# Summing the last expert group in PSUM and normalising the other rows while its experts run

## The chip, the cores and the metric

The kernel runs on one core of one Trainium2 chip. The metric is the device time of one execution in microseconds (us): 941.54 us in the median of three runs of the kernel before (938.84 to 943.46).

The core has five engines with instruction streams of their own. TensorE (PE, with its weight loads as PEld) multiplies matrices into PSUM, VectorE (DVE) and ScalarE (ACT) work on tiles, GpSimd (POOL) issues the gathers, scatters and adding stores, and SyncE (SP) issues the plain loads and stores. Sixteen DMA engines move the data.

## The reference, cut to what matters

One decoder layer: a mixer sub-layer, which the change leaves alone, and then a mixture of experts. A router sends each of the 512 tokens to one of four groups and, inside it, to two of the group's four experts. The expert outputs are summed with their gates, added to the scaled input of the sub-layer, and normalised.

```python
for e in range(N_EXPERTS):                      # 16 experts, 4 in each group
    hid = jax.nn.silu(t @ w_gate[e]) * (t @ w_up[e])
    out = out + gates[:, e:e + 1] * (hid @ w_down[e])
...
y = hierarchical_moe(h, ...)
x = layer_norm(DEEPNORM_ALPHA * x + (1.0 + gt2) * y, ln2_g[l], ln2_b[l])
```

## The kernel before, in words

After the mixer and the router, `h2d` in HBM holds the experts' input by token, and `moed` holds the scaled residual, to which the expert results are added. `body(e, t)` runs tile `t` of up to 64 tokens (H) of expert `e`. Tile 0 is always run. Tiles 1 and 2 stand behind branches on the expert's token count, which each engine reads from SBUF into a register (`values_load`, a TENSOR_LOAD on every engine).

One body, in the order in which it stands on each engine: `up` (32 matmuls, L1281), `hidden` (Silu on ACT, L1285, and a product on DVE, L1286), then the `down` product of the tile before (16 matmuls, L1296), scaled by gate and modulation on DVE (L1300) and sent by `add` as an indirect DMA that adds to rows of `moed` (L1301, POOL). `x_columns` transposes the gathered tokens of the next expert (L1176, copied out by ACT, L1177), `hidden_columns` transposes the hidden tile (L1290, copied out by DVE), and `tile_tokens` turns one-hot rows (`onehots`, L1146, DVE) by small matmuls (L1151, L1153) into the token indices of expert `e + 2` and gathers their rows (L1156, POOL). `in_order` keeps PE, DVE and ACT in the order of the code inside one body: an instruction that waits holds up all that stand behind it on its engine.

Weights come over SP's queue (L358) into a ring of 1 MB buffers, some three experts ahead. A skipped branch that would have issued DMAs from POOL is made up for by an instruction on POOL that raises those DMAs' semaphores (INC_SWDGE_SEM).

At the end, the last `down` is added to `moed`. SP waits for that and loads all of `moed` back (L1420). For each of four tiles of 128 rows, DVE takes the statistics (L218, L219), ACT a square root (L220), DVE and ACT scale (L1424, L1425), and POOL stores to `out` with an adding DMA (L1426): `out` had been filled with the bias `ln2_b` in the middle of the mixer (L776).

Of the kernel before, what the change touches and what calls it, by code (L numbers as in the profile page):

```python
# [107 lines left out]
def hybrid_layer(ctx: ExitStack, tc: tile.TileContext, A, out):  # L108
# [663 lines left out]
    with tc.issue_after(ws.issued.ins):  # L772
# [3 lines left out]
        nc.sync.dma_start(out[0], bass.AP(tensor=A["ln2_b"].tensor, offset=A["ln2_b"].offset, ap=[[0, S], [1, D]]))  # L776
# [365 lines left out]
    rkx = rtile("rkx", [P, NT])  # L1142

# [68 lines left out]
    def over_counts():  # L1212
        nc.vector.tensor_copy(cnt, pc[:, 0:16])
        nc.vector.tensor_copy(cnti[:, 0:16], cnt)
        for b in range(NB):
            nc.vector.tensor_scalar(ext[:, b, :], cnt, float((b + INL) * H) + 0.5, None, op0=ALU.is_gt)
        nc.vector.tensor_reduce(nov, ext, axis=AX.XY, op=ALU.add)
        nc.vector.tensor_copy(cnti[:, 16:17], nov)

# [77 lines left out]

    def add(bank, yo, ix, gw):

        nc.vector.scalar_tensor_tensor(yo, bank, gw, gt2h, op0=ALU.mult, op1=ALU.mult)  # L1300
# [4 lines left out]
    def body(e, t):  # L1305

        bank, by, yo, sg = bgu[t], bys[t % 2], yos[t % 2], sgs[t % 2]
        with in_order((ET.PE, ET.DVE, ET.Activation)):
            if t == 0:
# [3 lines left out]
                tile_ranks(e, 2)  # L1313
            if t == 1:
                tile_tokens(e, 2)
# [7 lines left out]
            if t:  # L1323
                down(ew, e, by)
                add(by, yo, ixs[e % 3][t - 1], gws[e % 3][t - 1])
            elif e:
                down(ew, e - 1, by)
                add(by, yo, ixl[1 - e % 2], gwl[1 - e % 2])
                ew.drop(2)
# [3 lines left out]
            if t == 1:  # L1333
                x_columns(xgs[e % 2, 2], xTs[e % 2, 2])
            hidden_columns(sg)
            if t == 0 and e + 2 < NE:
                for u in range(2):
                    tile_tokens(e + 2, u)

    n_toks = [nc.values_load(cnti[0:1, e:e + 1], min_val=0, max_val=S) for e in range(NE)]  # L1340
    n_over = nc.values_load(cnti[0:1, 16:17], min_val=0, max_val=MAXO)
    n_raw = len(ew.raws)
    assert n_raw >= 18

    for e in range(NE):
        body(e, 0)
        with tc.If(n_toks[e] > H):  # L1347
            body(e, 1)
            with tc.If(n_toks[e] > 2 * H):
                body(e, 2)  # L1350
        if e + 1 < NE:
            ew.drop(4)
    down(ew, NE - 1, bys[0])
    add(bys[0], yos[0], ixl[(NE - 1) % 2], gwl[(NE - 1) % 2])


    spare = [ew.piece(6 * (NE - 3) + n) for n in range(18)]
    ms, gs = ([spare[6 + 2 * a + i // 2][:, i % 2 * D:(i % 2 + 1) * D] for i in range(NT)] for a in range(2))
    ln2g = spare[10][:, 0:D]
    nc.sync.dma_start(ln2g, row_bcast(A["ln2_g"], D))  # L1360
# [52 lines left out]
    with ExitStack() as nest:  # L1413
        for t in range(MAXO):
            nest.enter_context(tc.If(n_over > t))
            over(t)


    for i in range(NT):
        nc.sync.dma_start(ms[i], moed[i * P:(i + 1) * P, :])  # L1420
    for i in range(NT):
        mv = ln_stats(ms[i], f"y{i}")
        nc.vector.tensor_scalar(mv[:, 3:4], mv[:, 0:1], -1.0, None, op0=ALU.mult)
        nc.vector.scalar_tensor_tensor(gs[i], ms[i], mv[:, 3:4], ln2g, op0=ALU.add, op1=ALU.mult)  # L1424
        nc.scalar.mul(gs[i], gs[i], mv[:, 2:3])  # L1425
        nc.gpsimd.dma_start(out[0, i * P:(i + 1) * P, :], gs[i], accum_op=ALU.add)  # L1426
# [25 lines left out]
```

## Time and profile before

| | |
|---|---|
| median of three runs | 941.54 us |
| the profiled execution | 941.18 us |
| its span, first to last instruction | 939.3 us |
| PE busy | 845.4 us (90%) |
| DVE busy | 534.7 us (57%) |
| ACT busy | 313.6 us (33%) |
| POOL busy | 105.8 us (11%) |
| mean granted clock of TensorE | 0.958 |

The span runs from the first to the last instruction of the profiled execution, and the 1.9 us between it and the execution's own time lie around it. Busy shares are means over stages of different kinds: until 901 us PE works almost without a break, and in the last 38 us it does nothing. The granted clock is given as a share of TensorE's full clock: 1.00 is 2.4 GHz and 0.50 is 1.2 GHz.

### The profile page before, as it was taken

Reading aid. Unit: us, or ns where it says so; the run is one execution under the profiler, and the core shown is the slowest. Engines: PE = TensorE matmul, PEld = TensorE weight load, DVE = VectorE, ACT = ScalarE, POOL = GpSimd, SP = SyncE. Lnnn points to the kernel's source line nnn. Section 1 sums busy time; section 2 is a strip of 40 time slices with the busy share of each in tenths; the row PEclk is TensorE's granted clock in tenths of the full one; section 3 lists DMA queues with packets and bytes.
Section 4 is the critical chain, followed back from the end, with each engine's and each line's share of the span. In section 5 each row is a group of like instructions: output and inputs, shape, how many; then the busy total and the mean of one; then the engine's idle time right before and its main releaser. Section 6 shows DMA issues by size and latency. Waiting matters only on the chain. (4 is left out here: it accounts for less than half of the span.)

```text
span 939.3 us, 11850 instructions
## 1 busy us (share of the span) xinstructions
PE 845.4 (90%) x4216; PEld 544.4 (58%) x4216; DVE 534.7 (57%) x1310; ACT 313.6 (33%) x561; POOL 105.8 (11%) x118
## 2 busy tenths in 40 slices
PE   2899989999999999999999994999999999999830
PEld 1678768887666677878888882433344333334310
DVE  6849879858876678876845773422342223232123
ACT  5438787454644433423234351101111000011002
POOL 1001000000000000000000022222231222121111
PEclk9899999999999999999999975999999999999975
DMA  9951456313125258894424399598799997549445
GB/s 288 339 142 52 154 175 183 90 35 102 46 68 161 90 169 267 247 291 147 176 94 178 135 348 381 210 375 290 273 388 387 381 359 273 189 136 367 155 123 103
DMA packets 137409, 196.46 MB, mean 209 GB/s; under 512 B 11802, under 2 KB 85706, under 8 KB 137312
## 3 DMA queue, kind: packets, MB, share of 16 engines
q1 hardware_dynamic: 126848, 174.28, 54.5%
q0 software_dynamic: 10304, 21.08, 9.1%
q8 instruction: 46, 0.75, 0.3%
q14 instruction: 35, 0.29, 0.1%
q10 hardware_dynamic: 176, 0.06, 0.0%
HBM read 190.61 MB, written 15.25 MB: 219 GB/s over the span
## 5 line engine op out<-in xcount | busy, mean ns | idle before, releaser
L398 PE MATMUL bank<-rm,rm 128*128 128x512 f32 x512 | 206.1, 406 | 0.4 <-ACT rm L431 0.4
L400 PE MATMUL bank<-rm,rm 128*128 128x512 f32 x512 | 205.9, 402 | 0.0
L399 PE MATMUL bank<-rm,rm 128*128 128x512 f32 x512 | 205.1, 401 | 0.2 <-DVE rm L433 0.2
L1281 PE MATMUL bank<-bm,fm 128*64 128x512 f32 x472 | 124.2, 597 | 1.8 <-PEq L1347 0.8
L234 DVE TENSOR_TENSOR rm<-fm,rm 128x1024 fp32r<-128x1024 f32 (+1 forms) x76 | 87.5, 1162 | 43.2 <-ACT rm L233 27.6
L398 PEld LDWEIGHTS bank<-rm,rm 128*128 128x128 f32 x512 | 97.8, 191 | 22.1 <-issue 3.1
L399 PEld LDWEIGHTS bank<-rm,rm 128*128 128x128 f32 x512 | 97.3, 190 | 21.7 <-issue 2.1
L400 PEld LDWEIGHTS bank<-rm,rm 128*128 128x128 f32 x512 | 97.2, 190 | 20.7 <-issue 2.3
L1286 DVE TENSOR_TENSOR fm<-fm,bank 64x512 f32<-64x512 f32 x24 | 16.6, 692 | 152.2 <-ACT fm L1285 143.2
L233 ACT CAST rm<-fm 128x1024 fp32r<-128x1024 f32 (+1 forms) x76 | 75.1, 1008 | 78.4 <-PE bank L399 59.4
L1281 PE MATMUL bank<-fm,fm 128*64 128x512 f32 x296 | 81.4, 610 | 3.8 <-issue 1.9
L1285 ACT ACTIVATE fm<-bank 64x512 f32<-64x512 f32 x24 | 14.1, 589 | 198.6 <-PE bank L1281 198.6
L1281 PEld LDWEIGHTS bank<-bm,fm 128*64 128x64 f32 x472 | 38.1, 136 | 66.7 <-issue 65.4
L1296 PE MATMUL bank<-bm,fm 128*64 128x512 f32 x232 | 60.4, 592 | 0.0
L390 DVE SCALAR_TENSOR_TENSOR fm<-fm,cact,fm 128x256 f32<-128x256 f32 x112 | 51.2, 479 | 1.8
L1177 ACT COPY fm<-bank 128x512 f32<-128x512 f32 x38 | 20.9, 588 | 87.9 <-PE bank L1176 87.7
L1281 PEld LDWEIGHTS bank<-fm,fm 128*64 128x64 f32 x296 | 24.7, 140 | 40.7 <-issue 39.0
L1300 DVE SCALAR_TENSOR_TENSOR fm<-bank,fm,fm 128x512 f32<-128x512 f32 x24 | 18.0, 750 | 47.7 <-PE bank L1296 42.7
L1002 PE MATMUL bank<-rm,rm 128*128 128x512 f32 x192 | 44.2, 391 | 0.3 <-ACT fm L847 0.3
L1301 POOL DMA_INDIRECT moed<-fm,rt_ixl x16 | 25.6, 1603 | 152.5 <-DVE fm L1300 143.1
L1156 POOL DMA_INDIRECT fm<-h2d,rt_ix x38 | 39.1, 1029 | 28.7 <-DVE fm L1160 20.6
L1002 PEld LDWEIGHTS bank<-rm,rm 128*128 128x128 f32 x192 | 36.0, 188 | 8.1 <-ACT fm L847 0.7
(312 smaller groups left out, 1102.7 us busy)
## 6 DMA issues: line engine op xcount, KB each, us to landing
bm<-in_w_down SPq DMA_DIRECT2D x20, 1024.0 KB, 13.7
bm<-in_w_up SPq DMA_DIRECT2D x20, 1024.0 KB, 12.3
bm<-in_w_gate SPq DMA_DIRECT2D x20, 1024.0 KB
fm<-in_w_in SPq DMA_DIRECT2D x36, 512.0 KB, 4.9
fm<-in_w_mod SPq DMA_DIRECT2D x16, 1024.0 KB, 5.3
fm<-in_w_up SPq DMA_DIRECT2D x12, 1024.0 KB, 16.1
fm<-in_w_down SPq DMA_DIRECT2D x12, 1024.0 KB, 14.4
fm<-in_w_gate SPq DMA_DIRECT2D x12, 1024.0 KB
```

Of the source, the lines that this page charges most:

```text
L233: ins = nc.scalar.copy(hi, src)
L234: nc.vector.tensor_tensor(lo, src, hi.bitcast(F32), op=ALU.subtract)
L390: nc.vector.scalar_tensor_tensor(acc, r, cact[:, k:k + 1], acc, op0=ALU.mult, op1=ALU.add)
L398: nc.tensor.matmul(pt, whi[:, k, :], ah.ap, start=(k == 0), stop=False)
L399: nc.tensor.matmul(pt, whi[:, k, :], al.ap, start=False, stop=False)
L400: nc.tensor.matmul(pt, wlo[:, k, :], ah.ap, start=False, stop=(k == nk - 1))
L1002: nc.tensor.matmul(wps[i][hf], sta.ap[:, tsl], mov.ap[:, hf * 512:(hf + 1) * 512], start=(k == 0 and sta is mh and mov is wh), stop=(k == ...
L1156: nc.gpsimd.indirect_dma_start(out=xg, out_offset=None, in_=h2d2, in_offset=bass.IndirectOffsetOnAxis(ap=ix[:, 0:1], axis=0), bounds_check ...
L1177: nc.scalar.copy(xT, pt)
L1281: nc.tensor.matmul(bank[n * H:(n + 1) * H], xT[:, (2 * (k % 4) + k // 4) * H:(2 * (k % 4) + k // 4 + 1) * H], w, start=(k == 0), stop=(k = ...
L1296: nc.tensor.matmul(bank[n * H:(n + 1) * H], hidT[0][:, k, :], w, start=(k == 0), stop=(k == 3))
L1301: nc.gpsimd.indirect_dma_start(out=moed2, in_=yo, in_offset=None, compute_op=ALU.add, out_offset=bass.IndirectOffsetOnAxis(ap=ix[:, 0:1], ...
```

## The change: what it does

A flag `n_one` is counted beside the others: no expert needs more than three tiles, and the last group (experts 12 to 15) has at most 128 tokens. After expert 11 every engine branches on it (L1571). Where it is 0, `general()` runs what was there before, except that the bias is added by DVE and `out` is written by plain stores. Where it is 1, `Rows` runs experts 12 to 15 in another way:

- `begin` clears two PSUM banks (two matmuls with a zero matrix) and makes one-hot rows of the group's tokens. `slots` multiplies these with an expert's one-hot rows into a 0/1 matrix from expert slots to group slots. `sum` multiplies it with the scaled expert output, so that the four experts' results add up in the two banks. These experts send nothing to `moed`.
- Before expert 14, `load` puts the rows of `moed`, the gain, the bias, and a gather of the group's own rows on POOL's queue. `norm` normalises two tiles of 128 rows at the start of expert 14's body and two at the start of expert 15's, and SP stores them to `out` plainly. The group's rows among them are wrong at that point.
- After expert 13, `end` makes `ixg`, the token indices of the group's rows, by five small matmuls and two operations on DVE.
- `ends` adds the banks to the group's gathered rows in two halves of 512 columns (on DVE, with the row sums), squares them (ACT), takes the square root (ACT), applies gain and bias by halves (DVE), and stores them over the others with one indirect DMA.

The early store of the bias to `out` goes. `x_columns` uses one PSUM bank in these experts, where two alternated, and the tiles are at most two for an expert.

```diff
-        nc.sync.dma_start(out[0], bass.AP(tensor=A["ln2_b"].tensor, offset=A["ln2_b"].offset, ap=[[0, S], [1, D]]))
...
+        nc.vector.tensor_scalar(one[:, 0:1], nov, 0.5, None, op0=ALU.is_le)
+        nc.vector.tensor_scalar(one[:, 1:2], cnt[:, 19:20], P + 0.5, one[:, 0:1], op0=ALU.is_le, op1=ALU.mult)
+        nc.vector.tensor_copy(cnti[:, 17:18], one[:, 1:2])
...
-                tile_ranks(e, 2)
+                if not rows:
+                    tile_ranks(e, 2)
-            if t == 1:
+            if rows:
+                rows.start(e, t)
+            elif t == 1:
                 tile_tokens(e, 2)
...
+                if summed:
+                    weigh(by, yo, gw)
+                else:
+                    add(by, yo, ix, gw)
...
-                for u in range(2):
-                    x_columns(xgs[1 - e % 2, u], xTs[1 - e % 2, u])
+                x_columns(xgs[1 - e % 2, 0], xTs[1 - e % 2, 0])
+                if rows:
+                    hidden_columns(sg)
+                x_columns(xgs[1 - e % 2, 1], xTs[1 - e % 2, 1])
...
+            if rows:
+                if summed:
+                    rows.sum(yo)
+                rows.slots(t)
...
+        def begin(self):
+            for a in (zerob, *slot):
+                nc.vector.memset(a, 0.0)
+            nc.vector.tensor_scalar(itg, itf, 1.0, None, op0=ALU.add)
+            onehots(self.ohg, rk[:, :, 19], itg)
+            for bank in self.acc:
+                nc.tensor.matmul(bank, zerob, self.ohg.rearrange("p c s -> p (c s)"), start=True, stop=False)
+        def start(self, e, t):
+            if (e, t) == (self.first, 0):
+                self.begin()
+            onehots(ohs[3 + t], rk[:, :, e], itbs[t])
+            if t == 0 and e >= NE - 2:
+                for i in (2 * (e - NE + 2), 2 * (e - NE + 2) + 1):
+                    self.norm(i)
+        def slots(self, t):
+            pt = bix[:, 256:256 + P]
+            for c in range(NT):
+                nc.tensor.matmul(pt, ohs[3 + t][:, c, :], self.ohg[:, c, :], start=(c == 0), stop=(c == NT - 1))
+            for hf in range(2):
+                nc.scalar.copy(slot[hf][hf * H:(hf + 1) * H], pt[hf * H:(hf + 1) * H])
+        def sum(self, yo, last=False):
+            for hf in range(2):
+                nc.tensor.matmul(self.acc[hf], slot[hf], yo, start=False, stop=last)
+...
+        def load(self):
+            for i in range(NT):
+                nc.gpsimd.dma_start(self.zs[i], moed[i * P:(i + 1) * P, :])
+            nc.gpsimd.dma_start(self.lng, row_bcast(A["ln2_g"], D))
+            nc.gpsimd.dma_start(self.lnb, row_bcast(A["ln2_b"], D))
+            nc.gpsimd.indirect_dma_start(out=self.x1, out_offset=None, in_=moed[:, :],
...
+        def norm(self, i):
+            z, v = self.zs[i], mvr[:, i, :]
+            nc.scalar.activation(self.junk, z, AF.Identity, accum_out=v[:, 0:1])
+            nc.vector.tensor_scalar(v[:, 1:2], v[:, 0:1], -1.0 / D, None, op0=ALU.mult)
+            nc.scalar.activation(self.junk, z, AF.Square, bias=v[:, 1:2], accum_out=v[:, 2:3])
+            nc.scalar.activation(v[:, 3:4], v[:, 2:3], AF.Sqrt, bias=epsc, scale=1.0 / D)
+            nc.vector.scalar_tensor_tensor(z, z, v[:, 1:2], self.lng, op0=ALU.add, op1=ALU.mult)
+            nc.vector.reciprocal(v[:, 4:5], v[:, 3:4])
+            nc.vector.scalar_tensor_tensor(z, z, v[:, 4:5], self.lnb, op0=ALU.mult, op1=ALU.add)
+            nc.sync.dma_start(out[0, i * P:(i + 1) * P, :], z)
+        def ends(self):
+            nc.scalar.activation(mvr[:, 2, 3:4], epsc, AF.Sqrt)
+            down(ew, NE - 1, by)
+            weigh(by, yo, gwl[(NE - 1) % 2])
+            self.sum(yo, True)
...
+            nc.gpsimd.indirect_dma_start(out=out[0], out_offset=bass.IndirectOffsetOnAxis(ap=ixg[:, 0:1], axis=0),
+                                         in_=y, in_offset=None, bounds_check=S - 1, oob_is_err=False)
...
+    for e in range(NE - 4):
+        expert(e, INL)
+    with tc.If(n_one > 0) as last:
...
+            tr.tiles = banks[3:4]
+            for e in range(NE - 4, NE):
+                if e == NE - 2:
+                    rows.load()
+                expert(e, 2, rows)
...
+                rows.ends()
+    with last.Else():
+        general()
```

The order in which instructions stand changes at three places. A row below names the line, the operation, what it writes and what it reads; `fm_` and `bm_` are buffers, `bank_` PSUM banks.

On DVE, between the last instruction of expert 11 (the copy of its hidden columns) and the Silu product of expert 12, this stood before:

```order
L1291 COPY fm_70<-bank_66 128x256
L1349 UNCONDITIONAL_BRANCH x2
L1347 UNCONDITIONAL_BRANCH
L1146 TENSOR_SCALAR fm_70<-fm_80 128x128 x5
L1286 TENSOR_TENSOR fm_78<-fm_78,bank_61 64x512
```

and stands now (L1298 is the copy, L1149 the one-hot rows, L1293 the product):

```order
L1298 COPY fm_70<-bank_66 128x256
L1375 UNCONDITIONAL_BRANCH x3
L1367 TENSOR_LOAD rt_cnti x4
L1368 TENSOR_LOAD rt_cnti
L1369 TENSOR_LOAD rt_cnti
L1571 COMPARE_AND_BRANCH
L1149 TENSOR_SCALAR fm_70<-fm_80 128x128 x8
L1474 MEMSET fm_80 128x64
L1474 MEMSET fm_80 128x128 x2
L1475 TENSOR_SCALAR fm_80<-itf 128x128
L1149 TENSOR_SCALAR fm_70<-fm_80 128x128 x8
L1293 TENSOR_TENSOR fm_78<-fm_78,bank_61 64x512
```

The six register loads, four of which stood at the later branches, now precede the branch, and of the last eight one-hot rows the first four are the group's, for which PE's two clearing matmuls (L1478) wait ahead of `up` of expert 12.

On POOL, the gathers of expert 15's tokens, then the branch of expert 13, stood so before:

```order
L1301 DMA moed<-fm_78,rt_ixl_3500 1280x512
L1156 DMA fm_75<-h2d,rt_ix_3491 128x512
L1156 DMA fm_74<-h2d,rt_ix_3492 128x512
L1340 TENSOR_LOAD rt_cnti
L1347 COMPARE_AND_BRANCH
```

and stand so now (ISA is the raising of a semaphore, L1511 the loads of `moed`):

```order
L1604 ISA
L1159 DMA fm_75<-h2d,rt_ix_3490 128x512
L1604 ISA
L1159 DMA fm_74<-h2d,rt_ix_3491 128x512
L1375 COMPARE_AND_BRANCH
L1375 UNCONDITIONAL_BRANCH x2
L1604 ISA
L1511 DMA fm_77<-moed 128x1024
L1604 ISA
L1511 DMA fm_77<-moed 128x1024
L1604 ISA
L1511 DMA bm_3752<-moed 128x1024 x2
```

The loads of `moed` stand behind the second gather, and each of the first three behind one more raise; gain, bias and the gather of the group's rows follow them.

On ACT, expert 14 had its Silu and the two copies of the columns of expert 15, ahead of the next branch:

```order
L1285 ACTIVATE fm_78<-bank_61 64x512
L1177 COPY fm_75<-bank_65 128x512
L1177 COPY fm_74<-bank_64 128x512
L1340 TENSOR_LOAD rt_cnti
L1347 COMPARE_AND_BRANCH
```

and has now, from the end of expert 13's branch on (L1520 to L1523 are `norm`, L1292 the Silu, L1180 the copies, L1494 those of `slots`):

```order
L1520 ACTIVATE bm_3754,fm_80<-fm_77 128x1024
L1522 ACTIVATE bm_3754,fm_80<-fm_77,fm_80 128x1024
L1523 ACT_TABLE_LOAD
L1523 ACTIVATE fm_80<-fm_80,epsc 128x1
L1520 ACTIVATE bm_3754,fm_80<-fm_77 128x1024
L1522 ACTIVATE bm_3754,fm_80<-fm_77,fm_80 128x1024
L1523 ACTIVATE fm_80<-fm_80,epsc 128x1
L1292 ACT_TABLE_LOAD
L1292 ACTIVATE fm_78<-bank_61 64x512
L1180 COPY fm_75<-bank_64 128x512
L1520 ACTIVATE bm_3754,fm_80<-bm_3752 128x1024
L1180 COPY fm_74<-bank_64 128x512
```

The Silu of expert 14 now stands behind the statistics of two tiles of `moed` and two loads of ACT's function table.

## Rows read from the trace of the kernel before

**Rows 1.** Fifty us: length, busy us (x instructions), granted clock, DMA share, GB/s.
```profile
850.00:900.00 50.00, 45.64 (x230) 19.59 (x228) 12.96 (x48) 6.61 (x11) 10.59 (x8) 1.00 0.65 231
```
**Rows 2.** Timeline of the end: start, us, engine, line, what, idle time before.
```profile
897.76 3.65 PE L1296 MATMUL bank<-fm,fm 128*64 128x512 f32 x16 [0.71 <-DVEq L1347]
...
902.55 0.75 DVE L1300 SCALAR_TENSOR_TENSOR fm<-bank,fm,fm 128x512 f32<-128x512 f32 x1 [4.97 <-DMA moed<-fm,rt_ixl]
...
913.43 1.29 DVE L218 BATCH_NORM_STATS2 st_y<-bm 128x6 f32<-128x512 f32 x2 [10.13 <-DMA bm<-moed]
...
925.93 0.85 POOL L1426 DMA_DIRECT2D out<-bm  x1 [0.85 <-ACT bm L1425]
```
**Rows 3.** Line 1448, the program's end: ns min/median/max, first and last start.
```profile
L1448 SPq DRAIN  x3: 7/7/7, 934.7 to 938.7; - x3
```
**Rows 4.** Windows of ACT's line 1285, the Silu, from 842.4 us on.
```profile
842.40:939.30 96.90, 2.35 (x4) 0.83 0.63 186
```
**Rows 5.** PE's line 681: products with 128 x 128 weights, 512 columns.
```profile
L681 PE MATMUL bank<-fm,ones 128*128 128x512 f32 x2 | 1.0, 592 | 0.0
```
**Rows 6.** Groups of ACT, shapes apart: shape, count, busy us, mean ns, idle before.
```profile
L1177 ACT COPY fm<-bank 128x512 f32<-128x512 f32 x38 | 20.9, 588 | 87.9 <-PE bank L1176 87.7
...
L1018 ACT ACTIVATE fm<-fm,mv 128x1024 f32<-128x1024 f32 x6 | 6.9, 1154 | 24.5 <-DVE mv L1017 24.5
...
L1019 ACT ACTIVATE mv<-mv,epsc 128x1 f32<-128x1 f32 x6 | 1.8, 294 | 0.2
...
L1285 ACT ACT_TABLE_LOAD x1 | 1.3, 1283 | 6.7 <-issue 6.7
...
L1018 ACT ACTIVATION_READ_ACCUMULATOR fm<-fm,mv 128x1 f32 x6 | 1.1, 184 | 0.0
```
**Rows 7.** A group of DVE, columns as in rows 6.
```profile
L1424 DVE SCALAR_TENSOR_TENSOR bm<-bm,mv_y,bm 128x1024 f32<-128x1024 f32 x4 | 5.1, 1274 | 0.0
```
**Rows 8.** DMA issues of the whole span: count, KB each, median us to landing.
```profile
moed<-fm POOLq DMA_DIRECT2D x4, 512.0 KB, 4.9
...
moed<-fm,rt_ixl POOLq DMA_INDIRECT x16, 8.1
```
**Rows 9.** Timeline at the start of expert 12, columns as in rows 2.
```profile
842.16 0.42 DVE L1291 COPY fm<-bank 128x256 f32<-128x256 f32 x1 [0.26 <-PE bank L1290]
...
842.54 6.65 PE L1281 MATMUL bank<-fm,fm 128*64 128x512 f32 x29 [0.42 <-PEq L1349]
...
842.92 0.91 DVE L1146 TENSOR_SCALAR fm<-fm 128x128 bf16<-128x128 bf16 x5 [0.34 <-DVEq L1349]
```
**Rows 10.** Line 1340, the register loads: ns min/median/max, first and last start.
```profile
L1340 DVEq TENSOR_LOAD <-rt_cnti x16: 299/304/554, 594.8 to 897.1; - x16
```
**Rows 11.** DVE's timeline at a branch with one such load.
```profile
883.97 0.74 DVE L1146 TENSOR_SCALAR fm<-fm 128x128 bf16<-128x128 bf16 x4 [0.71 <-PEq L1347]
```
**Rows 12.** PE's timeline at an earlier stop, after the routing.
```profile
579.10 2.09 PE L1176 MATMUL bank<-ident,fm 128*128 128x128 f32 x8 [10.66 <-DMA fm<-h2d,rt_ix]
581.12 5.91 PE L1281 MATMUL bank<-fm,fm 128*64 128x512 f32 x17
```
**Rows 13.** Windows around changes of the granted clock, columns as in rows 1.
```profile
905.00:906.00 1.00, 0.00 (x0) 0.00 (x0) 0.00 (x0) 0.00 (x0) 0.14 (x1) 0.85 0.55 33
...
582.00:584.00 2.00, 2.00 (x8) 0.71 (x6) 0.48 (x3) 1.42 (x3) 0.00 (x0) 0.50 1.03 392
...
586.00:588.00 2.00, 2.00 (x12) 0.71 (x10) 1.42 (x7) 0.00 (x0) 0.00 (x0) 1.00 0.17 61
```
**Rows 14.** PE's timeline in expert 14: first matmuls, columns of expert 15.
```profile
869.63 1.07 PE L1281 MATMUL bank<-bm,fm 128*64 128x512 f32 x2
...
881.26 1.09 PE L1176 MATMUL bank<-ident,fm 128*128 128x128 f32 x8
```
**Rows 15.** POOL's timeline: the last gather of expert 15.
```profile
871.54 1.00 POOL L1156 DMA_INDIRECT fm<-h2d,rt_ix  x1 [0.31 <-DVE fm L1146]
```
**Rows 16.** Line 1347, the branches: POOL's raises of semaphores, ns min/median/max.
```profile
L1347 POOLq INC_SWDGE_SEM  x10: 1043/1298/2027, 595.0 to 897.9; - x10
```

More of the change, by code (lines that the diff above doesn't have):

```diff
@@ L1142, in hybrid_layer @@
     rkx = rtile("rkx", [P, NT])
+    zerob, itg = rtile("zerob", [P, P], BF16), rtile("itg", [P, P], BF16)
+    slot = [rtile(f"slot{hf}", [P, P]) for hf in range(2)]
+    ixg, mvr = rtile("ixg", [P, 1], I32), rtile("mvr", [P, NT, 5])
+    ixf = rtile("ixf", [P, 1])
     def onehots(oh, ranks, slots):
@@ L1338, in body, with expert @@
                     tile_tokens(e + 2, u)
+            if rows:
+                rows.end(e, t)
     n_toks = [nc.values_load(cnti[0:1, e:e + 1], min_val=0, max_val=S) for e in range(NE)]
     n_over = nc.values_load(cnti[0:1, 16:17], min_val=0, max_val=MAXO)
+    n_one = nc.values_load(cnti[0:1, 17:18], min_val=0, max_val=1)
     n_raw = len(ew.raws)
     assert n_raw >= 18
[L1345 to L1350, printed above, removed]
+    def expert(e, tiles, rows=None):
+        body(e, 0, rows)
+        with ExitStack() as nest:
+            for t in range(1, tiles):
+                nest.enter_context(tc.If(n_toks[e] > t * H))
+                body(e, t, rows)
         if e + 1 < NE:
             ew.drop(4)
[L1353 to L1357 removed]
+    assert rtc[1] <= 4 * UNIT
+    spare = [ew.piece(6 * NE - 18 + n) for n in range(18)]
     ms, gs = ([spare[6 + 2 * a + i // 2][:, i % 2 * D:(i % 2 + 1) * D] for i in range(NT)] for a in range(2))
[L1359 to L1360 removed]
+    ln2g, lnb = spare[10][:, 0:D], spare[11][:, 0:D]
     rtc[:] = spare[10][:, D:2 * D], 0
@@ L1411, in over, with general @@
         add(bys[1], yos[1], ixs[0][0], gws[0][0])
[L1413 to L1426, printed above, removed]
+    def general():
+        for e in range(NE - 4, NE):
+            expert(e, INL)
+        nc.sync.dma_start(ln2g, row_bcast(A["ln2_g"], D))
+        down(ew, NE - 1, bys[0])
+        add(bys[0], yos[0], ixl[(NE - 1) % 2], gwl[(NE - 1) % 2])
+        with ExitStack() as nest:
+            for t in range(MAXO):
+                nest.enter_context(tc.If(n_over > t))
+                over(t)
+        nc.sync.dma_start(lnb, row_bcast(A["ln2_b"], D))
+        for i in range(NT):
+            nc.sync.dma_start(ms[i], moed[i * P:(i + 1) * P, :])
+        for i in range(NT):
+            mv = ln_stats(ms[i], f"y{i}")
+            nc.vector.tensor_scalar(mv[:, 3:4], mv[:, 0:1], -1.0, None, op0=ALU.mult)
+            nc.vector.scalar_tensor_tensor(gs[i], ms[i], mv[:, 3:4], ln2g, op0=ALU.add, op1=ALU.mult)
+            nc.vector.scalar_tensor_tensor(gs[i], gs[i], mv[:, 2:3], lnb, op0=ALU.mult, op1=ALU.add)
+            nc.sync.dma_start(out[0, i * P:(i + 1) * P, :], gs[i])
@@ new lines, in arm @@
+    @contextmanager
+    def arm():
+        state = ew.nload, ew.ndrop, tr.tiles, tr.i
+        yield
+        ew.nload, ew.ndrop, tr.tiles, tr.i = state
+    for e in range(NE - 4):
+        expert(e, INL)
+    with tc.If(n_one > 0) as last:
+        with arm():
+            rows = Rows()
+            tr.tiles = banks[3:4]
+            for e in range(NE - 4, NE):
+                if e == NE - 2:
+                    rows.load()
+                expert(e, 2, rows)
+            with in_order((ET.PE, ET.DVE, ET.Activation)):
+                rows.ends()
```

77 lines of the change are left out of this document (61 added, 16 removed).

## The prediction, made before the changed kernel had run

> **What bounds the kernel now.** I read the stages first. In the window from 850 to 900 us PE is busy for 45.64 of 50 us, and the other engines for far less [rows 1]: as long as the experts run, the time is what PE does and each stop of PE. Then I read the timeline of the end. PE's last `down` begins at 897.76 and ends at 901.41; the product that weighs it waits until 902.55 for the adding store before it; the statistics start at 913.43, after an adding store and a load of all rows; the last store to `out` is issued at 925.93 [rows 2]. SP's drain, which waits for that store to land, comes at 934.7, and the span ends at 939.3 [rows 3]. So 37.9 us lie behind PE's last matmul: 24.5 to the issue of the last store, 8.8 to its landing, 4.6 for the program's end. Last I asked which side of the branch runs: from 842.4 us on there are four Silu [rows 4], so each of the experts 12 to 15 ran tile 0 alone, with at most 64 tokens. Each token has two experts in its group, so the group has at most 4 x 64 / 2 = 128 tokens, and the new path is taken.
>
> **The tail, the gain.** From PE's last matmul on, the new chain is: weigh 0.75, which no adding store holds up now, with 0.10 to start; two products of `sum`, 0.59 each [rows 5], to 1.95; bank plus residual by halves on DVE, each like the weighing, 0.75 [rows 2], to 3.4; the square of a half on ACT, half of 1.15 and 0.18 for its sum, to about 4.3; a load of ACT's function table, 1.28, since the Silu of expert 15 stands between the early Sqrt and this one, and the Sqrt itself, 0.29, to 5.9 [rows 6]; reciprocal and two halves of a product, 1.27 together [rows 7], to 7.5. Then POOL stores. So 24.5 becomes 7.5: -17.0. The store is 512 KB, not adding; the plain 512 KB write of POOL's queue landed in 4.9 us, the indirect adding one in 8.1 [rows 8]. I take 4.9, being plain, in place of 8.8: -3.9; with 8.1 it is -0.7. The 4.6 of the end stay. Together -20.9, bounds -17.7 and (the table load hidden, the chain 2 us shorter) -24.
>
> **The entry, a cost.** Expert 12's first matmul is at 842.54, just behind the last instruction of expert 11, and DVE's five one-hot rows (0.91 for five, 0.18 each) are beside it [rows 9]. Now PE's two clearing matmuls stand ahead of `up` and need the group's one-hot rows. On DVE come first six register loads, of 0.30 each by themselves [rows 10]; DVE's gap at a branch is 0.71 with one such load [rows 11] and 0.34 without [rows 9], so 0.37 each, 2.2. Then eight one-hot rows 1.5, three small clears and one operation about 0.6, four more one-hot rows 0.75, and the clearing, about 0.4: from 842.58, where the copy ends, to 848.0, and `up` at 848.5. +6.0; with overlapped register loads 3.5, with each step a little longer 7.
>
> A stop of PE costs a second time. At the end the granted clock was 0.85 in the microsecond from 905 on, four after the last matmul; after an earlier stop of 10.66 us [rows 12] it was 0.50 from 582 to 584 and 1.00 from 586 on [rows 13]. At the low level 17 matmuls took 5.91 us [rows 12], at the full one 29 took 6.65 [rows 9], 0.229 each: 17 would take 3.9, and the part of the low stretch ahead of them loses a little over 1. So +3.1 for a stop of 6 us, and nothing if the clock holds through it.
>
> **Experts 12 and 13, a cost.** Each has four matmuls for `slots` with their copies on ACT into the matrix, ahead of the matmuls of `tile_tokens`, which use the same bank (`bix`): about 0.45 on PE, and about 0.9 until both copies are done. The second `x_columns` waits for the copy of the first out of the one bank, 0.59 [rows 6], of which most but not all lies beside the hidden columns; 0.85 with the signals. That is +2.2 in expert 12. Expert 13 has the two products of `sum` too, 1.0, and five matmuls for `ixg`, 0.5: +3.7. Together +5.9; 3 if PE finds all copies done, 8 if each is waited for.
>
> **Expert 14, the largest cost.** Let S be PE's first matmul of expert 14, 869.63 before. The columns of expert 15 follow at 881.26, eight transposes in 1.09 [rows 14]; in the new order the hidden columns of expert 14 come after four of them, at S + 12.2. They need its Silu, and on ACT that stands behind the sums, squares and roots of two tiles of `moed`. When can these be done? POOL issued the last gather for expert 15 at 871.54, for 1.00 [rows 15], so it was free at S + 2.9. In the new listing one raise more stands between the two gathers and one behind them, of 1.30 each [rows 16]: 5.5, less 0.5, since PE's matmuls for `ixg` put S off against the gathers. So the first load of `moed` is issued at S + 5.0 and lands, by the 4.9 of rows 8, at 9.9. Four more issues of 0.9 and two raises of 1.3 later the gain is issued, at 11.2, and lands at 16.1, the bias at 17.0. ACT has summed (1.15 + 0.18) and squared (the same) the first tile by then [rows 6]. DVE waits for the gain: product 1.27 [rows 7], reciprocal, product with the bias, to 18.9. Only then comes its small product with the second tile's sum, which ACT's next square needs: 19.1, square to 20.4, root 20.7, table load for Silu 22.0, Silu 22.6, product 23.3. PE stops from 12.2 to 23.4, or 11.2; with raises at their least, 1.04 [rows 16], and issues that overlap, about 10. I take +10.0. Were gain and bias there as early as the tiles, 4; with loads that land in 8.1 and not in 4.9, 13. The clock then costs again, about 2.8. The two tiles of expert 15 (their data landed long before) need some 7 us, and its Silu is wanted after 12: nothing.
>
> The Trainium skill bears on that landing: "DMA: Bandwidth & Descriptors", section "Anatomy of one DMA — SWDGE (gpsimd) path", has a fixed part of about 2.0 us and bytes at 436 GB/s beside it. As an estimate by this page 512 KB land in 3.2 us, where the row has 4.9; the stop would be 1.7 shorter, and the sum 948.1.
>
> **The rest.** Experts 14 and 15 have `sum` and `slots` too, 1.5 and 1.3: +2.8. Four register loads that stood at later branches are gone, about 0.25 each on PE's way: -1.0. The early store of the bias lay beside PE's work in the mixer, and three more small operations of the counts lie beside PE's wait of 10.66 us for the gather [rows 12]: both 0. Four adding stores go, which PE did not wait for: 0.
>
> **The sum**, against the profiled execution's 941.18 us (its span 939.3 and 1.9 around it; 0.36 below the median of 941.54): -20.9 + 6.0 + 3.1 + 5.9 + 10.0 + 2.8 + 2.8 - 1.0 = +8.7, so 949.8 us. With the terms' bounds moving apart, 943 to 957.
>
> **The rivals.**
> *No stop in expert 14.* The loads come early enough that ACT is done by S + 12.2. For it: DMA has room once the last weights are in, and DVE and ACT are mostly idle in this stage [rows 1]. Against it: even with data at S + 9.9, four passes over the tiles at 1.33, two Sqrt and two table loads do not fit into 2.3. Without the stop and its clock, 12.8 go: 937.0, some 4 below the kernel before. It ends faster by more than the bound where the tail gives back all of its 24 us (934), or the body terms are at their low ends.
>
> *A short stop.* Gain and bias land with the tiles; PE stops for 4 and the clock holds. 6.0 and 2.8 go: 941.0, no change.
>
> *Dearer.* The five loads and the gather, 3.5 MB in one queue, slow one another as the adding stores do (8.1 for 512 KB, rows 8), and PE waits beyond 13 in expert 14, or the bodies reach their 8: 957 to 961.
>
> *Not what it says.* If the counts sent the kernel to the other side of the branch, only plain stores in place of adding ones and a product on DVE in place of ACT's would be left, with the six register loads at the entry: about 941 to 944.
>
> A rule of the skill counts against the change here. Rows: one table load is 1.28 [rows 6], and the new order alternates Sqrt and Silu in experts 14 and 15, two of whose loads, the one to Silu in 14 and the one at the tail, are on PE's or the end's path in my sum. "ScalarE: Activation LUTs", section "Table sets: the hidden batching unit", says to batch activations by set, and its section "What ACT_TABLE_LOAD costs" adds a drain of about 1.38 us to every switch; no row shows a drain beside a load, and by the page, as an estimate, the sum would be 952.6.
>
> **How the numbers follow.** About 0.5% (4.7 us) is what a measurement of this kernel can tell from no change. The forecast has 0.47 (slower by over that bound 0.42, within it 0.05); no stop 0.25 (faster 0.16, within 0.09); a short stop 0.15 (within 0.13, slower 0.02); dearer 0.10, all slower; the other side of the branch 0.03, within. Faster 0.16, same 0.30, slower 0.54. The forecast's own range is 943 to 957. The range takes in the short stop and most of the no-stop case, and leaves out some 0.1 below and 0.1 above: 936 to 957.
>
> **What would show it.** In the changed profile: PE idle for about 6 us ahead of the clearing matmuls, then a granted clock of 0.50; in expert 14 PE idle for about 10 us at the hidden columns, released by DVE or ACT, with the Silu behind squares of `moed` tiles and DVE's first gain product waiting for a DMA; about 7.5 us from the last `down` to POOL's store, with one table load between; four Silu after the branch. The prediction is wrong if PE goes through expert 14 without a stop of 4 us or more, if the clock holds at 1.00 through both stops, or if the store at the end lands in 8 us and the rest is as said.

## The result and the profile after

The changed kernel takes 950.05 us (median of 4 runs, 947.92 to 950.53) and the kernel before 940.19 beside it (937.57 to 943.46): a ratio of 1.0103, 95% interval 1.0082 to 1.0123. Forecast were 949.8 us and slower. Against the kernel before beside it the change costs 9.9 us, where +8.7 was forecast from a base of 941.18. The profiled execution of 949.85 us has a span of 947.8, 8.5 longer than before.

The entry to the last four experts on PE's timeline (start, us, instruction, idle time before it and what ended it), which answers to [rows 9]:

```profile
846.46 1.01 PE L1478 MATMUL bank<-fm,fm 128*128 128x512 bf16 x2 [6.02 <-DVE fm L1149]
847.39 9.60 PE L1288 MATMUL bank<-fm,fm 128*64 128x512 f32 x32
```

PE stands for 6.02 us, released by DVE's one-hot rows, and then `up` takes 9.60 us. DVE beside it:

```profile
840.47 0.42 DVE L1298 COPY fm<-bank 128x256 f32<-128x256 f32 x1 [0.26 <-PE bank L1297]
...
843.73 1.39 DVE L1149 TENSOR_SCALAR fm<-fm 128x128 bf16<-128x128 bf16 x8 [2.83 <-issue]
...
845.59 1.39 DVE L1149 TENSOR_SCALAR fm<-fm 128x128 bf16<-128x128 bf16 x8
```

The copy that ends expert 11 is over at 840.89 (842.58 before); 2.83 us of register loads and branch follow, then eight rows of other experts, and the group's four, for which PE waits, are in the last piece. Before, PE ran `up` beside such rows; now `up` stands behind them. Windows of the same profile (length, busy us of each engine, granted clock, DMA share, GB/s) show both low stretches, as [rows 13] did:

```profile
848.00:850.00 2.00, 2.00 (x6) 0.47 (x4) 0.00 (x0) 0.00 (x0) 0.00 (x0) 0.50 1.05 331
...
854.00:856.00 2.00, 2.00 (x12) 0.59 (x10) 0.00 (x0) 0.00 (x0) 0.00 (x0) 1.00 0.59 229
...
907.00:909.00 2.00, 2.00 (x4) 0.97 (x4) 0.00 (x0) 0.58 (x1) 0.00 (x0) 0.50 0.00 0
```

Expert 14, PE first, then the others, all in the changed kernel:

```profile
891.59 0.66 PE L1179 MATMUL bank<-ident,fm 128*128 128x128 f32 x4
905.20 1.12 PE L1297 MATMUL bank<-ident,fm 128*128 128x128 f32 x4 [12.96 <-DVE fm L1293]
```

```profile
884.90 0.59 POOL L1511 DMA_DIRECT2D fm<-moed  x1 [1.24 <-DMA fm<-h2d,rt_ix]
...
889.66 1.06 ACT L1520 ACTIVATE bm<-fm 128x1024 f32<-128x1024 f32 x1 [10.12 <-DMA fm<-moed]
...
889.99 0.53 POOL L1512 DMA_DIRECT2D bm<-in_ln_g  x1
...
892.29 1.28 ACT L1523 ACT_TABLE_LOAD   x1
893.59 0.29 ACT L1523 ACTIVATE fm<-fm,epsc 128x1 f32<-128x1 f32 x1
...
897.70 1.28 DVE L1524 SCALAR_TENSOR_TENSOR fm<-fm,fm,bm 128x1024 f32<-128x1024 f32 x1 [6.70 <-DMA bm<-in_ln_g]
...
900.47 1.15 ACT L1522 ACTIVATE bm<-fm,fm 128x1024 f32<-128x1024 f32 x1 [5.55 <-DVE fm L1521]
...
902.06 1.28 ACT L1292 ACT_TABLE_LOAD   x1
...
903.35 0.59 ACT L1292 ACTIVATE fm<-bank 64x512 f32<-64x512 f32 x1
...
904.46 0.69 DVE L1293 TENSOR_TENSOR fm<-fm,bank 64x512 f32<-64x512 f32 x1
```

Read from below: PE waits for the product (L1293), this for the Silu, that for a table load and the second tile's square (L1522) on ACT; the square waits 5.55 us for DVE, DVE 6.70 us for the gain, and the gain was issued at 889.99, fifth on POOL. `up` of expert 14 had ended at about 888: the Silu could have run 15 us earlier.

The tail, which answers to [rows 2, 3]:

```profile
925.90 3.65 PE L1303 MATMUL bank<-fm,fm 128*64 128x512 f32 x16 [0.30 <-PEq L1375]
...
930.49 1.96 PE L1498 MATMUL bank<-fm,fm 128*128 128x512 f32 x4 [0.94 <-DVE fm L1306]
...
935.01 1.28 ACT L1553 ACT_TABLE_LOAD   x1 [0.79 <-DVE fm L1552]
...
938.53 1.02 POOL L1559 DMA_INDIRECT out<-bm,rt_ixg  x1 [46.14 <-DVE bm L1557]
```

```profile
L1604 SPq DRAIN  x3: 7/7/7, 943.4 to 947.2; - x3
```

From the end of the last `down`, 929.55, to the store's issue there are 9.0 us (24.5 before), to its landing 4.9 (8.8), to the end 4.4 (4.6): 18.3 in place of 37.9.

The two profiles side by side, cut at four points of PE's work:

| | before | after | difference | forecast |
|---|---|---|---|---|
| end of expert 11's copy to `up` of expert 12 | 0.0 | 6.5 | +6.5 | +6.0 |
| from there to four column transposes in expert 14 (clock's first loss inside) | 39.3 | 44.9 | +5.6 | +8.5 |
| stop ahead of the hidden columns of expert 14 | 0 | 13.0 | +13.0 | +10.0 |
| from there to the last `down`, its start (clock's second loss inside) | 15.9 | 20.7 | +4.8 | +5.1 |
| last `down`, its end, to the end | 37.9 | 18.3 | -19.6 | -20.9 |

In the kernel before, the four transposes are taken as half of the eight in [rows 14]. The rows give +10.3; the changed run was 1.7 ahead when it came to the branch, which leaves, but for rounding, the 8.5 of the spans.

### The profile page after: what moved, and what is told of

The parts are those of the page before. It is cut to its first block, busy times and chain, and to the rows that moved or that the text cites. A ratio compares the mean times of both kernels' runs of the same rounds, so it can differ in the third digit from the quotient of the medians.

```text
span 947.8 us, 11967 instructions
## 1 busy us (share of the span) xinstructions
PE 856.1 (90%) x4255; PEld 545.2 (58%) x4255; DVE 542.3 (57%) x1330; ACT 327.8 (35%) x591; POOL 101.0 (11%) x118
## 5 line engine op out<-in xcount | busy, mean ns | idle before, releaser
L400 PEld LDWEIGHTS bank<-rm,rm 128*128 128x128 f32 x512 | 96.8, 189 | 20.7 <-issue 2.3
L1293 DVE TENSOR_TENSOR fm<-fm,bank 64x512 f32<-64x512 f32 x24 | 16.6, 692 | 139.6 <-ACT fm L1292 139.4
L1292 ACT ACTIVATE fm<-bank 64x512 f32<-64x512 f32 x24 | 14.1, 588 | 188.0 <-PE bank L1288 187.9
L1288 PEld LDWEIGHTS bank<-bm,fm 128*64 128x64 f32 x472 | 37.9, 136 | 62.1 <-issue 60.9
L1180 ACT COPY fm<-bank 128x512 f32<-128x512 f32 x38 | 21.1, 588 | 87.5 <-PE bank L1179 87.4
L1288 PEld LDWEIGHTS bank<-fm,fm 128*64 128x64 f32 x296 | 24.5, 143 | 43.4 <-issue 41.6
L1149 DVE TENSOR_SCALAR fm<-fm 128x128 bf16<-128x128 bf16 x196 | 37.2, 260 | 14.6 <-PE bank L1492 6.2
```

What stands on the lines that cost most here:

```text
L400: nc.tensor.matmul(pt, wlo[:, k, :], ah.ap, start=False, stop=(k == nk - 1))
L1149: nc.vector.tensor_scalar(oh[:, c, :], slots, ranks[:, c:c + 1], None, op0=ALU.is_equal)
L1180: nc.scalar.copy(xT, pt)
L1288: nc.tensor.matmul(bank[n * H:(n + 1) * H], xT[:, (2 * (k % 4) + k // 4) * H:(2 * (k % 4) + k // 4 + 1) * H], w, start=(k == 0), stop=(k = ...
```

## The experiments

The change has a gain and two costs, says the theory: a shorter tail, and two stops of PE, each of which costs a second time by the clock. Each is timed beside the kernel before on the same chip (ratios with 95% intervals); the changed kernel has 1.0103 (1.0082 to 1.0123).

| run | median us | beside | ratio |
|---|---|---|---|
| e1, one-hot rows behind the Silu product | 944.61 | 938.80 | 1.0072 (1.0047 to 1.0097) |
| e2, norms of expert 14 at its end | 941.47 | 938.80 | 1.0024 (1.0010 to 1.0038) |
| e3, gain and bias first | 949.01 | 938.80 | 1.0112 (1.0079 to 1.0144) |
| e4, loads over SP's queue | 944.47 | 938.80 | 1.0057 (1.0037 to 1.0078) |
| e5, matmuls added in the stops, 55 and 125 | 947.52 | 939.51 | 1.0080 (1.0057 to 1.0104) |
| e8, the same, 55 and 215 | 946.24 | 939.55 | 1.0070 (1.0043 to 1.0097) |
| e7, the general side | 942.62 | 939.51 | 1.0026 (1.0012 to 1.0040) |
| e6, parts put together | 929.80 | 939.51 | 0.9901 (0.9882 to 0.9920) |
| e10, e6 with the sides swapped | 938.37 | 939.40 | 0.9987 (0.9972 to 1.0003) |

**The entry (e1).**

```diff
-            if (e, t) == (self.first, 0):
-                self.begin()
...
             nc.vector.tensor_copy(gwl[e % 2], gws[e % 3][t])
+            if rows and (e, t) == (rows.first, 0):
+                rows.begin()
...
+                if (e, t) == (rows.first, 0):
+                    rows.clear()
                 rows.slots(t)
```

> The group's one-hot rows and clears move behind the Silu product of expert 12 on DVE, the two clearing matmuls behind its hidden columns on PE. Theory (PE waits at the entry because its clearing matmuls stand ahead of the first `up`): the stop of 6.0 us in the changed kernel shrinks to the register loads on PE itself, about 2 us, the clock holds, and the 2.3 us that 32 matmuls lost at the low level come back: 950.0 - 4 - 2.3 = about 943.5 us. Rival (the entry is held by the branch, its six register loads and the code behind it, not by the one-hot rows): PE still stands for 5 us or more ahead of `up`, and the time stays within 949 to 951.

PE's timeline at the entry of this run, and its clock:

```profile
843.40 7.09 PE L1288 MATMUL bank<-fm,fm 128*64 128x512 f32 x32 [3.09 <-issue]
```

```profile
842.00:846.00 4.00, 2.60 (x13) 1.09 (x15) 2.04 (x12) 0.00 (x0) 0.00 (x0) 1.00 0.88 275
```

The stop is 3.09, not 6.02, the clock stays, and the same 32 matmuls take 7.09 in place of 9.60. That is 5.4 us in the trace, as in the medians (950.05 to 944.61); by the ratios it is 0.3%, 3 us, and their intervals overlap, so that the trace is the better witness. The theory holds; what is left, 3.09, is more than the 2 expected. In PE's own stream only the six register loads and the branch stand there.

**Where the norms stand (e2).**

```diff
-            if t == 0 and e >= NE - 2:
+            if t == 0 and e == NE - 1:
...
                 rows.slots(t)
+                if (e, t) == (NE - 2, 0):
+                    rows.norm(0)
+                    rows.norm(1)
```

> The two `norm` of expert 14 move from the start of its body to its end; those of expert 15 stay. Theory (Silu of expert 14 stands behind them on ACT, and this is the whole stop of 13.0 us): PE goes through expert 14 without a stop, 13 and the clock's 2.8 us go; the norms of four tiles now stand ahead of the Silu of expert 15, where a stop of 2 to 6 us comes up: 937 to 941 us. Rival (the loads of `moed` on POOL or their traffic hold PE, whoever waits for them): a stop of 8 us or more stays in expert 14 or 15, and the time is above 945.

PE's only long stop behind the entry is in expert 15:

```profile
911.56 1.11 PE L1297 MATMUL bank<-ident,fm 128*128 128x128 f32 x4 [6.45 <-DVE fm L1293]
```

With the same loads at the same place PE goes through expert 14, so the loads held it only through the norms. The four tiles one behind the other now hold the Silu of expert 15, for 6.45 us. The time fell by 0.8%, some 7 us, and not by 13.0 and the clock's share, because the new stop takes a part back; both the stop (2 to 6 expected) and the 941.47 us (937 to 941) lie just outside what was expected.

**Which load (e3).**

```diff
+            nc.gpsimd.dma_start(self.lng, row_bcast(A["ln2_g"], D))
+            nc.gpsimd.dma_start(self.lnb, row_bcast(A["ln2_b"], D))
             for i in range(NT):
                 nc.gpsimd.dma_start(self.zs[i], moed[i * P:(i + 1) * P, :])
-            nc.gpsimd.dma_start(self.lng, row_bcast(A["ln2_g"], D))
-            nc.gpsimd.dma_start(self.lnb, row_bcast(A["ln2_b"], D))
```

> POOL issues gain and bias ahead of the four tiles of `moed`; all else as in the changed kernel. Theory (DVE's wait for the gain, the fifth load, sets the second half of the stop, since the second tile's mean stands behind it on DVE): gain and bias land before the tiles, the chain of two tiles ends some 3 us earlier, stop of 10 instead of 13, about 947 us. Rival (ACT's sums, squares and table loads set it alone, or the first tile's landing): the stop stays at 13 or grows by the two issues ahead of the first tile, 950 to 952.

POOL, ACT and PE in this run:

```profile
889.78 1.05 POOL L1513 DMA_DIRECT2D fm<-moed  x2 [0.80 <-issue]
```

```profile
895.14 1.06 ACT L1520 ACTIVATE bm<-fm 128x1024 f32<-128x1024 f32 x1 [14.83 <-DMA fm<-moed]
```

```profile
905.70 1.12 PE L1297 MATMUL bank<-ident,fm 128*128 128x128 f32 x4 [12.69 <-DVE fm L1293]
```

DVE waits for the gain no more, but the first tile is issued at 889.78 in place of 884.90, and ACT begins 5.5 us later: a stop of 12.69. The rival was right: the two issues on POOL, the raise between them and the traffic stand ahead of the tiles then, and one wait took the place of the other. The run also prices the chain by itself: from the first tile's work on ACT to PE's hidden columns it takes 10.6 us here (895.14 to 905.70), and 15.5 in the changed kernel (889.66 to 905.20). So of the stop of 13.0 about 5 are the wait for the gain, and about 8 would be left, as an estimate, were the gain there with the first tile.

**Which queue (e4).**

```diff
-                nc.gpsimd.dma_start(self.zs[i], moed[i * P:(i + 1) * P, :])
-            nc.gpsimd.dma_start(self.lng, row_bcast(A["ln2_g"], D))
-            nc.gpsimd.dma_start(self.lnb, row_bcast(A["ln2_b"], D))
+                nc.sync.dma_start(self.zs[i], moed[i * P:(i + 1) * P, :])
+            nc.sync.dma_start(self.lng, row_bcast(A["ln2_g"], D))
+            nc.sync.dma_start(self.lnb, row_bcast(A["ln2_b"], D))
```

> The four tiles of `moed`, gain and bias are loaded over SP's queue in place of POOL's; order of ACT, DVE and PE as in the changed kernel. SP has issued its last weights at 873.7 us there, 11 us before POOL issues the first of these loads. Theory (the stop in expert 14 is lateness of the loads, on POOL behind the gathers and raises of semaphores): tiles and gain land about 10 us earlier, the stop falls to 0 to 4 us, the clock holds: 934 to 940 us. Rival (the stop is ACT's and DVE's own work, 10 us whenever it begins): ACT and DVE begin earlier but PE still stops for 8 us or more, above 945. Rival 2 (the loads collide with the last weights): PE waits for weights in expert 14 or 15 instead, by 3 us or more.

SP's wait in this run (line waited for, us in total, times, longest), its issue of the gain and DVE's wait for it, and PE:

```profile
SPq L1511 <- PEq L1375: 9.7, 1, 9.7
```

```profile
884.68 0.51 SPq L1512 DMA_DIRECT2D bm<-in_ln_g  x1
...
894.37 1.28 DVE L1524 SCALAR_TENSOR_TENSOR fm<-fm,fm,bm 128x1024 f32<-128x1024 f32 x1 [6.30 <-DMA bm<-in_ln_g]
```

```profile
901.88 1.12 PE L1297 MATMUL bank<-ident,fm 128*128 128x128 f32 x4 [10.54 <-DVE fm L1293]
```

SP was free, as I had said, but waited 9.7 us for PE to pass the branch of expert 13 (L1375). The first tile's ACT work began at 886.73, only 2.9 us earlier. DVE waited for the gain again: issued at 884.68, it was there at 894.37, after 9.7 us, where it had needed 7.7 on POOL's queue. Measured against PE's own work (the four column transposes start at 890.68 here and at 891.59 in the changed kernel) the gain came 2.4 us earlier, and the stop shrank by 2.4, from 12.96 to 10.54. So the lateness of the gain counts one for one. The theory, which had the loads land 10 us earlier, missed a wait that the branch brings and a slower landing. The stop of 8 or more that the first rival foresaw is there, but not for its reason, ACT's and DVE's own work; the second rival (a collision with the weights) did not show.

**The clock (e5, e8).**

```diff
+        def warm(self, n):
+            for i in range(n):
+                nc.tensor.matmul(bgu[1][:, 0:P], onesb, onesb, start=(i == 0), stop=(i == n - 1))
+
         def begin(self):
+            self.warm(55)
...
                 if rows:
+                    if e == NE - 2:
+                        rows.warm(125)
                     hidden_columns(sg)
```

> Matmuls whose results nobody reads are added on PE where it stands still in the changed kernel: 55 small ones ahead of the two clears at the entry, 125 ahead of the hidden columns of expert 14. No wait is changed. Theory (each stop costs a second time, because PE comes out of it at the granted clock of 0.50): the clock stays at 1.00, the 32 matmuls of `up` in expert 12 take 7.3 instead of 9.6 us, the columns, sums and slots behind the stop in expert 14 some 2.8 less: about 945 us, with PE's last `down` some 5 us earlier. Rival (the matmuls behind a stop are slow for another reason, such as weights that are still landing, or the lost time is won back at the next wait): no change, 949 to 951.

> As the run with the added matmuls, with 215 in place of 125 of them ahead of the hidden columns of expert 14: there 125 took 7.14 us and PE stood another 6.33 behind them, so that the clock fell all the same. Theory: with 12.3 us of them PE comes out of the stop at 1.00, columns, sums and slots behind it take 2.8 us less, and the time is some 5 below the changed kernel's 950.05: about 945. Rival (what stands behind the stop waits for DVE and ACT, not for PE's speed): no gain over the 947.5 of the run with 125.

PE's timeline in e5, and then in e8:

```profile
841.41 4.79 PE L1476 MATMUL bank<-fm 128*128 128x128 bf16 x55 [3.18 <-issue]
...
846.64 7.09 PE L1288 MATMUL bank<-fm,fm 128*64 128x512 f32 x32
...
888.81 7.14 PE L1476 MATMUL bank<-fm 128*128 128x128 bf16 x125
902.28 1.12 PE L1297 MATMUL bank<-ident,fm 128*128 128x128 f32 x4 [6.33 <-DVE fm L1293]
```

```profile
891.66 12.17 PE L1476 MATMUL bank<-fm 128*128 128x128 bf16 x215
904.40 0.66 PE L1297 MATMUL bank<-ident,fm 128*128 128x128 f32 x4 [0.58 <-DVE fm L1293]
...
907.57 1.07 PE L1288 MATMUL bank<-bm,fm 128*64 128x512 f32 x2
```

Windows of e5 at the entry, then of e8 in expert 14:

```profile
844.00:846.00 2.00, 2.00 (x21) 2.00 (x20) 0.74 (x5) 0.00 (x0) 0.00 (x0) 0.50 1.03 284
846.00:848.00 2.00, 1.85 (x11) 0.66 (x12) 0.00 (x0) 0.00 (x0) 0.00 (x0) 0.95 1.05 344
```

```profile
902.00:906.00 4.00, 3.42 (x43) 2.84 (x41) 3.58 (x8) 3.23 (x6) 0.00 (x0) 1.00 0.35 139
```

At the entry the clock fell after all, while the added matmuls ran, but in both runs it was back soon after `up` began, and `up` took 7.09 us; in expert 14, in e5, the 125 matmuls filled half of the stop, the clock fell behind them, and the columns took 1.12 as in the changed kernel. In e8, 215 of them filled it, the last row has 1.00, and from the hidden columns to `up` of expert 15 it took 3.17 us, where the changed kernel took 5.57 (905.20 to 910.77). So the two losses are 2.5 and 2.4 us. The times of the two runs give no more than the direction: the changed kernel's interval overlaps both, and at the entry the 55 matmuls ran longer than the wait, so that `up` began 7.9 us (e5) and 9.1 us (e8) after the copy that ends expert 11, against 6.5 in the changed kernel. That took back 1.4 us of the gain in e5 and 2.6 in e8.

**The other side of the branch (e7).**

```diff
-        nc.vector.tensor_scalar(one[:, 1:2], cnt[:, 19:20], P + 0.5, one[:, 0:1], op0=ALU.is_le, op1=ALU.mult)
+        nc.vector.tensor_scalar(one[:, 1:2], cnt[:, 19:20], 0.5, one[:, 0:1], op0=ALU.is_le, op1=ALU.mult)
```

> The flag's bound on the last group is put at 0, so that the other side of the branch runs, with the last four experts as before; what is left of the change is the branch with its six register loads, the bias added on DVE and plain stores to `out` by SP. Theory: PE is held some 2 us by the loads at the entry, the adding stores' landing falls from 8.8 to about 5 us, the early store of the bias was hidden: 938 to 941, within 0.5% of the kernel before. Rival (the early store of the bias or the adding stores cost the kernel before 5 us or more by themselves, and the sums in PSUM gain less): 935 or below.

PE's entry and its last `down` in this run, and SP's drain at its end:

```profile
850.96 9.95 PE L1288 MATMUL bank<-fm,fm 128*64 128x512 f32 x32 [9.82 <-issue]
...
905.83 3.65 PE L1303 MATMUL bank<-fm,fm 128*64 128x512 f32 x16 [0.64 <-DVEq L1375]
```

```profile
L1604 SPq DRAIN  x3: 7/7/7, 940.4 to 940.7; - x3
```

From the end of that `down`, 909.48, to the end of its span of 941.3 there are 31.8 us, 6.1 fewer than before: plain stores and the bias on DVE are worth that much alone. The last store is issued at 937.6, 28.1 us behind the `down` (24.5 before), because gain and bias both stand on DVE; its landing and the program's end take 3.7 (13.4 before). In the changed kernel that chain is 9.0, and so 15.5 of its 19.6 are of a kind that this side does not have: they belong to the sum in PSUM and the early norms together, which no run parts. The run is slower than before, by 0.26% with an interval clear of 1, and its 942.62 us lie above the 938 to 941 expected (and far from the rival's 935), because PE stood for 9.82 us at the entry and `up` ran 9.95 behind it.

**Swapping the sides (e10, on e6).** In the changed kernel the general code lies behind the new path's.

```diff
-    with tc.If(n_one > 0) as last:
+    with tc.If(n_one < 1) as last:
+        with arm():
+            general()
+    with last.Else():
         with arm():
             rows = Rows()
...
-    with last.Else():
-        general()
```

> The kernel that puts the parts together (929.8 us), with the two sides of the branch in the other order in the program: the general code first, the new path behind it. What is computed and the order on each engine stay. In the run that took the general side, placed behind the other, PE stood for 9.8 us at the entry and not 3.1, with 5 packets on the instruction queues and not 1. Theory (a jump over the other side's code to instructions that have to be fetched costs 6 to 7 us at the entry, and the clock falls then): the new path starts with a stop of 9 to 10 us, time 929.8 + 6.7 + 2.5 = about 939. Rival (the 9.8 us belong to what the general side does at its start): the stop stays at 3.1 and the time at 930.

PE's and DVE's timeline and the DMA queues from 838 to 852 us (packets, MB, share) in this run, and the queues in e6:

```profile
848.60 2.04 DVE L1149 TENSOR_SCALAR fm<-fm 128x128 bf16<-128x128 bf16 x12 [8.84 <-issue]
...
849.93 9.82 PE L1288 MATMUL bank<-fm,fm 128*64 128x512 f32 x32 [10.64 <-DVE fm L1149]
```

```profile
q14 instruction: 8, 0.07, 1.2%
q8 instruction: 1, 0.02, 0.5%
```

```profile
q8 instruction: 1, 0.02, 0.4%
q14 instruction: 2, 0.02, 0.4%
```

The stop is 10.64 in place of 3.11, with 9 packets on the instruction queues in place of 3, and the time 938.37, as the theory had it: the stop goes with the place of the code and not with what it does. DVE itself stood for 8.84 us there, against 2.84 in e6. (The single packet of the expectation had been counted over a shorter window; over this one the changed kernel with the edit of e1 has 3.) That the time goes into fetching instructions fits the packets, but no run shows it directly. (In a build before this one, e9, the general side came first without `arm`, so that the new path took other weight buffers than meant and does not compute the layer; it had 938.07.)

**Put together (e6).** The edit of e1, that of e4, and:

```diff
                 rows.slots(t)
+                if (e, t) == (NE - 2, 0):
+                    for i in range(3):
+                        rows.norm(i)
+                elif (e, t) == (NE - 1, 0):
+                    rows.norm(3)
...
-            nc.scalar.activation(mvr[:, 2, 3:4], epsc, AF.Sqrt)
```

> The parts that gained are put together: the group's one-hot rows and clears behind the Silu product of expert 12, the loads of `moed`, gain and bias over SP's queue, and `norm` of three tiles at the end of the body of expert 14 and of the fourth at the end of that of expert 15, where its Sqrt takes the place of the early one. Theory (the change loses at two stops of PE, and its tail gains): neither stop is left, but one of 0 to 4 us in expert 15, and the load of the function table in the tail is gone: 927 to 934 us, below the kernel before. Rival (ACT and DVE have not the room for four tiles beside PE's work, wherever they are put): a stop of 5 us or more comes up in expert 15, or in the tail, and the time is 935 or more.

PE's stops at the entry and around the last `down`, a window of the last `sum`, then the tail:

```profile
841.70 7.09 PE L1288 MATMUL bank<-fm,fm 128*64 128x512 f32 x32 [3.11 <-issue]
...
904.81 3.65 PE L1303 MATMUL bank<-fm,fm 128*64 128x512 f32 x16 [2.03 <-DVEq L1384]
910.43 2.86 PE L1504 MATMUL bank<-fm,fm 128*128 128x512 f32 x4 [1.96 <-DVE fm L1306]
```

```profile
912.00:914.00 2.00, 1.29 (x2) 0.00 (x0) 1.15 (x5) 0.81 (x2) 0.00 (x0) 0.50 0.67 264
```

```profile
915.87 0.29 ACT L1558 ACTIVATE fm<-fm 128x1 f32<-128x1 f32 x1 [0.81 <-DVE fm L1557]
...
918.42 1.03 POOL L1564 DMA_INDIRECT out<-bm,rt_ixg  x1 [40.03 <-DVE bm L1562]
```

No stop is left in experts 14 and 15; there is one of 2.03 ahead of the last `down`, and the fourth tile's norm on DVE holds the last weighing for about 1. From the last `down`'s end, 908.46, to the store there are 10.0 us in place of 9.0, though the Sqrt needs no table load: the weighing is 1.0 later, and behind that wait the clock falls to 0.50, so that `sum` takes 2.86 and not 1.96. 929.80 us, 1.0% below the kernel before: with the stops away the tail's gain shows.

## Why the prediction was right

- *Bound and path*: PE's stops set the time and four Silu ran in the new path. Right.
- *Tail*, -20.9: -19.6. The landing was 4.9, as taken. (The 8.1 of [rows 8], the other bound, belongs to stores of 128 x 512 f32, which is 256 KB and not 512.) The chain was 9.0 and not 7.5. About half of the 1.5 is ACT's wait of 0.79 ahead of the table load for three small operations on DVE, which the chain had at nothing. Another misreading is of `sum`: a product of 128 x 128 f32 weights and 512 columns is two instructions in the trace, so that `sum` has four and takes 1.96, where I read the two rows of [rows 5] as two products. In the tail DVE's first half hides most of that; in each of experts 13 to 15 it is 0.9 more on PE than in the sum.
- *Entry*, +6.0: 6.5 by PE's timeline, and e1 takes the mechanism away. Register loads and branch took DVE 2.83; forecast were 2.2.
- *Clock*, +3.1 and +2.8: 2.5 and 2.4, shown by e1, e5 and e8 against the changed kernel.
- *Experts 12 and 13*, +5.9, less two register loads and with the clock 8.5: 5.6. This step was too dear. The second `x_columns` waited 0.29 for the copy, not 0.85, and PE ran the first matmuls of the next `up` between the token products, so that the copies of `slots` held nobody. The longer products of `sum` hid part of the error.
- *Expert 14*, +10.0: 13.0, at the upper bound. The order of the waits was as worked out, the first tile landed in 4.8 us (884.90 to 889.66), but the gain, fifth of six loads, needed 7.7 (889.99 to 897.70) where I put 4.9. It is its place in the queue that did this, and not the reading of one row for each partition: issued first, in e3, it landed in 4.4. This is the slowing that *Dearer* named, short of the 957 to 961 put on it. "No stop", the only rival on the faster side, falls with the stop in the changed kernel's own trace; e6 shows that it needed norms that stand elsewhere. "A short stop" was priced too low. From its data at S + 9.9, the passes, roots and table loads that "No stop" counts (8.5), the Silu and the product (1.3) lead to S + 19.7, a stop of 7.5 and not 4; by e3 it would be about 8.
- *The pages*: by the fit in the Trainium skill, "DMA: Bandwidth & Descriptors", section "Anatomy of one DMA — SWDGE (gpsimd) path", 512 KB land, as an estimate, in 3.2 us. The measured 4.8 and 7.7 decide against it here, where other loads are under way. The Trainium skill, "ScalarE: Activation LUTs", section "What ACT_TABLE_LOAD costs", adds a drain to each load. The trace has none: the load at 892.29 ends at 893.57 and the Sqrt starts at 893.59. The Trainium skill, "ScalarE: Activation LUTs", section "Table sets: the hidden batching unit", asks for batches by set. The trace agrees that a change of set costs a load, at 1.28 us: one of them stands ahead of the Silu of expert 14, on PE's way, and one in the tail.

That the total came within 0.3 us is luck: the stop was 3.0 dearer than forecast and the tail gained 1.3 less, experts 12 and 13 with the first clock loss cost 2.9 less, and the profiled run was 1.7 ahead at the branch. The 1.7 can be scatter: in the changed kernel and the nine runs of the table, whose code is the same up to there, the copy that ends expert 11 is over between 838.7 and 841.6. Whether the early bias store that is gone has a share in it stays open; it was not tried alone.

## What to carry to other kernels

Work that is moved off the tail into a busy stage is free only where no instruction of that stage is queued behind it: look on each engine for what comes next in order (here Silu behind two norms, `up` behind two clears), and add up when its data can be there. A stop of the engine that bounds is paid twice when its clock falls in it (here 2.5 us behind a stop of 6.0 and 2.4 behind one of 13.0). Of a branch, price the register loads, the meeting of the queues, and which side lies next in the program.

## What the runs showed of the hardware

- The side of the branch that lies behind the other cost a stop of PE of 9.8 us (e7) and 10.6 (e10), where the side that lies next cost 3.1 (e1, e6), with 5 and 9 packets on the instruction queues against 3.
- Behind a stop of 3.1 us the granted clock stayed at 1.00 where `up` followed (e1, e6) and fell to 0.50 where the added 128 x 128 matmuls followed a stop of 3.2 (e5, e8); after the stops of 6.0 and 13.0 us it was 0.50.
- The load of a row to all 128 partitions, 512 KB, took 7.1 and 7.5 us to land behind four tiles on POOL's queue (e2, e1), 9.7 to use behind them on SP's (e4), and 4.4 ahead of them on POOL's (e3).
- Around the load of ACT's function table no drain shows: it took 1.28 us, began 0.01 us behind the instruction before it, and the Sqrt behind it began 0.02 us after its end (changed kernel, 892.29).
